# Output projection of a hybrid layer: eight whole tiles in place of a seven-product Strassen scheme

## The chip, the cores and the metric

The kernel runs on one core of one Trainium2 chip. Its time is the device time of one execution in microseconds (us); the number compared is the median of several executions. The profile shows one execution.

## What is computed

One layer on a sequence of 1024 positions and 1024 channels. What matters here is the middle of it:

```python
merged = gates[:, :, 0, :] * y_pool + gates[:, :, 1, :] * y_lru
h = h + merged @ w_out[i]                              # 1024 x 1024 x 1024
v = rms_norm(h, norm2_g[i])
g_ff, u_ff = jnp.split(v @ w_ffn_in[i], 2, axis=-1)    # D_FF = 2816
h = h + (jax.nn.silu(g_ff) * u_ff) @ w_ffn_out[i]
```

Before it stand the input projection, a pooling branch and a recurrent branch (RG-LRU), each projected to 1024 channels; after it a gated embedding and a last norm. The matrices are float32.

## The kernel before

**Operands.** Channels lie on the 128 partitions, positions along the row: an activation of 1024 channels is eight tiles of 128x1024. To keep float32 accuracy each operand x of a product is split into a rounded part (`hi`, a cast on ScalarE, line 115) and the rest (`lo`, a subtraction on VectorE, line 119), both 512 wide in one tile, and a product is three matmuls: rounded by rounded, rounded by rest, rest by rounded (`mm3`, lines 219 to 221; `mm6`, line 227, does the same for the two halves of the positions, six matmuls with each weight block used for two banks).

**Two ways to multiply.** `plain` (line 840) makes one output tile at a time: for each of the eight input tiles an `mm6`, 48 matmuls, in two units of 24, into two PSUM banks that `done` evicts. `strassen` (line 419) takes output tiles in pairs and both halves of the positions, and makes of the 2x2 blocks seven products (Winograd's form) in place of eight: 84 matmuls for a pair where `plain` has 96. It pays with sums: the operands of the weights S1 to S4 come from four subtractions or additions for each pair (line 194), those of the activations T1, T2 and T4 from lines 400 to 406, and each of the seven products has weight and activation operands of its own, that is a cast and a subtraction each. A product is added to what the others left in its bank; the evictions (`Plain`, lines 484 to 512) copy or add parts into two tiles z, which the residual then adds to x.

**Who uses which.** The input projection, the output projection, and both matrices of the SwiGLU use `strassen`; the projections of the two branches and the gate of the embedding use `plain`. In the output projection the four pairs stand in two groups of two (line 987), and each product is made for both pairs of a group before the next product. The products come in the order 1, 5, 6, 2, 7, 3, 4, for which the activation operands are B11, T1, T2, B21, T3, B22, T4.

**Order.** All engines run the order in which the program is written down, by units (one product, or half an output tile). `drive` (line 276) writes a unit after the results of the unit before it (`post`), and prepares weight operands three units ahead, loads some more. Small jobs (`background`) get a share of each unit's time. TensorE, VectorE, ScalarE and the DMA queue of SyncE each work through their own list in order and wait for each other through semaphores.

**Around the change.** `done_lru` (line 930) closes an output tile of the recurrent branch's projection: it multiplies the two banks by the gate (line 933), adds the pooling branch (934) and puts the jobs for the activation operands of the output projection in the background (937, 940). `residual` (967) closes an output tile of the output projection: adds it to x (970), stores h (88), scales it to v (974), puts the jobs for the SwiGLU's activation operands B11, T1 and T2 in the background (977, 980), and squares h on ScalarE (327) to add it to the sum of squares (328). The tiles come out in the order 0, 2, 1, 3, 4, 6, 5, 7, the last four at the end of the second group. The SwiGLU's first product needs B11 of the tiles 0, 2, 4, 6; its second T1 of the same; its third T2, for which the odd tiles are needed too. After the first product TensorE adds up the squares (345), from which VectorE and ScalarE make the norm (350 to 356, 1001, 1002); after the fourth the norm is spread over the partitions (367). The first group of the SwiGLU has three pairs, so each of its products is 3 x 12 = 36 matmuls. Tiles live in one pool of 51 buffers (line 29); a load or cast that takes over a buffer waits for its last reader.

Of the kernel before, what the change touches and what calls it, by code (L numbers as in the profile page):

```python
# [19 lines left out]
KD = D // P  # L20
# [44 lines left out]
def hybrid_block(ctx: ExitStack, tc: tile.TileContext, xT, pT, vec, w_in, w_rgig, w_pool,  # L65
# [165 lines left out]
    background = deque()  # L231
# [686 lines left out]

    ma = Acts()

# [9 lines left out]
    def done_lru(m, banks):  # L930
        g = gate_of.pop(8 + m)
        for b, s in zip(banks, (LOW, HIGH)):
            dve.tensor_mul(g[:, s], g[:, s], b)
        dve.tensor_add(g, g, t0.pop(m))
        if m % 2 == 0:
            ma.a[m // 2] = g
            background.append(some_operands(ma, m // 2, ("B11", "T1")))
        else:
            ma.b[m // 2] = g
            background.append(some_operands(ma, m // 2, ("T2", "B21")))  # L940

# [10 lines left out]

    prepare_m = prepare(ma)

    def loads_of_group(m0):
        def pre(q, j, size):
            i = QS.index(q)
            if m0 == 0:
                if i == 0 and j == 0:
                    state["ss2"] = at("ss")  # L960
                    state["rep1"] = norm1.spread()
                prepare_m(q, j, size)
            if j == 0 and i in (2, 3, 4, 5):
                load_xr(m0 + {2: 0, 3: 2, 4: 1, 5: 3}[i])
        return pre

    def residual(m):
        def then(z):
            h = xr.pop(m)
            dve.tensor_add(h, h, z)  # L970
            store(h_spill[m], h)

            v = at("v")
            dve.scalar_tensor_tensor(v, h, col(C_G2, m), state["rep1"], ALU.mult, ALU.mult)  # L974
            if m % 2 == 0:
                va.a[m // 2] = v
                background.append(some_operands(va, m // 2, ("B11", "T1")))
            else:
                va.b[m // 2] = v
                background.append(some_operands(va, m // 2, ("T2",)))  # L980
            add_square(h, state["ss2"], m == 0)
            if m == KD - 1:
                state["norm2"] = Rstd(state["ss2"])
        return then

    strassen(ma, [(w_out[2 * i], w_out[2 * i + 1]) for i in range(KD // 2)],
             lambda i: Plain(residual(2 * i), residual(2 * i + 1)), loads_of_group(0),
             last=loads_of_group(4), groups=[2, 2])


# [295 lines left out]
```

## Time and profile before

| | |
|---|---|
| median of three runs | 1426.54 us (1425.07 to 1426.93) |
| the profiled execution | 1428.4 us |
| its span, first to last instruction | 1426.7 us |
| mean granted TensorE clock | 0.978 |
| TensorE busy | 1363.4 us (96%), 5958 matmuls |
| VectorE busy | 1074.8 us (75%) |
| ScalarE busy | 697.7 us (49%) |

In the profile PE is TensorE, PEld its weight loads, DVE VectorE, ACT ScalarE, POOL GpSimd, SP SyncE with its DMA queue. L119 is line 119 of the kernel. Busy time is the sum of the instructions' spans; those of matmuls overlap, since the next one starts before the last has drained, so the pace of matmuls is read from start to start. "Idle before" an instruction is the time its engine did nothing before it, with the engine and line whose end released it. The granted clock is the share of TensorE's full 2.4 GHz; the other level is half, 1.2 GHz.

### The profile page before, as it was taken

What the parts mean: (1) busy time and instruction counts of PE and PEld (TensorE: products, weight loads), DVE (VectorE), ACT (ScalarE), POOL (GpSimd) and SP (SyncE); (2) the same over time, 40 slices, a digit from 0 to 9 for tenths busy, and PEclk for the clock granted to TensorE, in tenths of its full rate; (3) what the DMA queues carried; (4) which work ended last, traced back from release to release, by engine and by line L of the source; (5) the groups of instructions that cost most, each with busy time, mean ns of one, the idle gap of its engine ahead of it and who ended that gap; (6) DMA issues with size and microseconds to landing.
All of it is one profiled execution on the core that took longest, in us unless ns stands there. A gap on an engine that the chain in (4) does not pass through costs nothing.

```text
span 1426.7 us, 16476 instructions
## 1 busy us (share of the span) xinstructions
PE 1363.4 (96%) x5958; PEld 1117.1 (78%) x5958; DVE 1074.8 (75%) x1583; ACT 697.7 (49%) x1114; POOL 86.5 (6%) x194
## 2 busy tenths in 40 slices
PE   6999999999999999977999999999999999999986
PEld 4787888888788888756788888888888877887865
DVE  5977788888775556778798888888787856768566
ACT  6558665877866122443554444444444521226331
POOL 0003010010000000000001000111110100000000
PEclk7999999999999999989999999999999999999997
DMA  7122143333559221332024444444567798813103
GB/s 311 74 78 97 58 153 110 122 124 109 193 197 364 89 89 38 110 138 98 16 89 148 148 162 148 162 163 163 192 233 268 277 419 303 343 66 126 62 28 118
DMA packets 64738, 220.56 MB, mean 155 GB/s; under 512 B 7312, under 2 KB 9872, under 8 KB 64656
## 3 DMA queue, kind: packets, MB, share of 16 engines
q1 hardware_dynamic: 45936, 151.80, 30.0%
q0 software_dynamic: 18576, 67.64, 11.7%
q8 instruction: 47, 0.77, 0.2%
q14 instruction: 35, 0.29, 0.1%
q10 hardware_dynamic: 144, 0.06, 0.0%
HBM read 147.65 MB, written 71.83 MB: 154 GB/s over the span
## 4 chain that ended last, share of the span: by engine, by line
PE 78%; DVE 11%; ACT 5%; issue 3%; DMA 2%; POOL 1%; DVEq 0%; SPq 0%; ACTq 0%; POOLq 0%
PE ps L221 22%; PE ps L220 22%; PE ps L219 22%; PE ps L227 11%; DVE w L119 2%; DVE ss L328 1%; DVE v L974 1%; DMA wr<-w_fout 1%; DVE xr L970 1%; DMA lT<-fT 1%; DVE wr L194 1%; PE ps L367 1%; DVE xB L119 1%; ACT w L115 1%; DVE xT L119 1%
## 5 line engine op out<-in xcount | busy, mean ns | idle before, releaser
L115 ACT CAST w<-wr 128x512 fp32r<-128x512 f32 (+2 forms) x384 | 227.1, 609 | 362.6 <-DVE wr L194 252.2
L119 DVE TENSOR_TENSOR w<-wr,w 128x512 fp32r<-128x512 f32 (+2 forms) x384 | 256.5, 672 | 52.6 <-ACT w L115 51.9
L221 PE MATMUL ps<-xT,w 128*128 128x512 f32 x704 | 276.3, 392 | 9.9 <-DVE w L119 9.9
L220 PE MATMUL ps<-xT,w 128*128 128x512 f32 x704 | 275.9, 392 | 3.4 <-DVE xT L119 3.4
L219 PE MATMUL ps<-xT,w 128*128 128x512 f32 x704 | 276.0, 392 | 0.1
L220 PE MATMUL ps<-xB,w 128*128 128x512 f32 x528 | 207.6, 393 | 9.3 <-DVE xB L119 9.1
L219 PE MATMUL ps<-xB,w 128*128 128x512 f32 x528 | 206.7, 392 | 2.1 <-ACT xB L115 1.2
L221 PE MATMUL ps<-xB,w 128*128 128x512 f32 x528 | 206.9, 392 | 0.0
L221 PEld LDWEIGHTS ps<-xT,w 128*128 128x128 f32 x704 | 133.1, 189 | 40.3 <-DVE w L119 12.7
L220 PEld LDWEIGHTS ps<-xT,w 128*128 128x128 f32 x704 | 133.1, 189 | 32.5 <-DVE xT L119 5.0
L219 PEld LDWEIGHTS ps<-xT,w 128*128 128x128 f32 x704 | 133.1, 189 | 28.4 <-ACT w L115 0.7
L220 PEld LDWEIGHTS ps<-xB,w 128*128 128x128 f32 x528 | 99.8, 189 | 32.2 <-DVE xB L119 11.8
L219 PEld LDWEIGHTS ps<-xB,w 128*128 128x128 f32 x528 | 99.8, 189 | 23.8 <-ACT xB L115 1.6
L221 PEld LDWEIGHTS ps<-xB,w 128*128 128x128 f32 x528 | 100.0, 189 | 21.1 <-DVE w L119 0.6
L227 PE MATMUL ps<-y,w 128*128 128x512 f32 x384 | 87.2, 389 | 0.0
L227 PEld LDWEIGHTS ps<-y,w 128*128 128x128 f32 x384 | 72.1, 188 | 15.0
L1079 DVE TENSOR_TENSOR h<-h,ps 128x512 f32<-128x512 f32 x68 | 46.5, 684 | 42.6 <-PE ps L221 42.4
L194 DVE TENSOR_TENSOR wr<-wr 128x512 f32<-128x512 f32 (+1 forms) x112 | 76.0, 679 | 3.1 <-DMA wr<-w_fout 1.1
L219 PE MATMUL ps<-lT,w 128*128 128x512 f32 x176 | 68.9, 392 | 3.4 <-DMA lT<-fT 2.6
L221 PE MATMUL ps<-lT,w 128*128 128x512 f32 x176 | 68.7, 390 | 0.0
L220 PE MATMUL ps<-lT,w 128*128 128x512 f32 x176 | 68.5, 389 | 0.0
L115 ACT CAST w<-s 128x512 fp32r<-128x512 f32 (+1 forms) x56 | 34.3, 613 | 57.3 <-DVE s L194 57.3
(218 smaller groups left out, 2145.0 us busy)
## 6 DMA issues: line engine op xcount, KB each, us to landing
wr<-w_fin SPq DMA_DIRECT2D x44, 512.0 KB, 5.7
fT<-xT POOLq DMA_DIRECT2D x44, 512.0 KB, 5.2
lT<-fT SPq DMA_DIRECT2D x44, 512.0 KB, 8.7
wr<-w_in SPq DMA_DIRECT2D x36, 512.0 KB, 4.1
fB<-xB POOLq DMA_DIRECT2D x33, 512.0 KB, 5.7
lB<-fB SPq DMA_DIRECT2D x33, 512.0 KB, 7.7
g<-z POOLq DMA_DIRECT2D x16, 512.0 KB, 2.9
g<-g SPq DMA_DIRECT2D x16, 512.0 KB, 6.4
```

Of the source, the lines that this page charges most:

```text
L115: act.copy(op[:, :x.shape[1]], x)
L119: dve.tensor_tensor(op[:, H:H + n], x, op[:, :n].bitcast(F32), ALU.subtract)
L194: f(self.place(out), self.place(a), self.place(b))
L219: pe.matmul(bank, a, xop[:, :H], start=first, stop=False, skip_group_check=more)
L220: pe.matmul(bank, a, xop[:, H:], start=False, stop=False, skip_group_check=more)
L221: pe.matmul(bank, b, xop[:, :H], start=False, stop=last, skip_group_check=more)
L227: pe.matmul(bank, w, xop[:, s], start=f, stop=e)
L328: dve.tensor_add(ss, ss, sq)
L367: pe.matmul(bank[:, i * P:(i + 1) * P], r[:, b + i:b + i + 1].broadcast_to([P, P]), ident, start=True, stop=True)
L970: dve.tensor_add(h, h, z)
L974: dve.scalar_tensor_tensor(v, h, col(C_G2, m), state["rep1"], ALU.mult, ALU.mult)
L1079: dve.tensor_add(h[t][:, s], h[t][:, s], bank)
```

## The change

The output projection goes through `plain`: eight output tiles, one after the other (the first two interleaved by halves), eight `mm6` each, 384 matmuls. Its input tiles get their two operands (one for each half of the positions) in `done_lru` as soon as they are made (`split`). `residual` takes the two banks and adds them straight to x; the tiles come out in the order 0 to 7, so that the pairs of neighbours of which the SwiGLU's operands are made are complete one after another. The tiles of x are loaded one output tile ahead. The weights of the output projection are laid out by whole tiles in place of pairs.

```diff
--- before.py
+++ after.py
@@ -916,7 +916,7 @@
     plain([w_pproj[m] for m in range(KD)], NG, lambda: mixed, done_pproj, pre_pproj)
 
 
-    ma = Acts()
+    ms = {}
 
     def pre_lru(m, a):
         if m == 0 and a == 0:
@@ -932,12 +932,7 @@
         for b, s in zip(banks, (LOW, HIGH)):
             dve.tensor_mul(g[:, s], g[:, s], b)
         dve.tensor_add(g, g, t0.pop(m))
-        if m % 2 == 0:
-            ma.a[m // 2] = g
-            background.append(some_operands(ma, m // 2, ("B11", "T1")))
-        else:
-            ma.b[m // 2] = g
-            background.append(some_operands(ma, m // 2, ("T2", "B21")))
+        ms[m] = split(g, "m")
 
     plain([w_lru[m] for m in range(KD)], KD, lambda: ys, done_lru, pre_lru, 2)
 
@@ -950,24 +945,20 @@
         xr[m] = at("xr")
         nc.sync.dma_start(xr[m], xT[m])
 
-    prepare_m = prepare(ma)
-
-    def loads_of_group(m0):
-        def pre(q, j, size):
-            i = QS.index(q)
-            if m0 == 0:
-                if i == 0 and j == 0:
-                    state["ss2"] = at("ss")
-                    state["rep1"] = norm1.spread()
-                prepare_m(q, j, size)
-            if j == 0 and i in (2, 3, 4, 5):
-                load_xr(m0 + {2: 0, 3: 2, 4: 1, 5: 3}[i])
-        return pre
+    def pre_out(m, a):
+        if a == 0:
+            if m == 0:
+                state["ss2"] = at("ss")
+                state["rep1"] = norm1.spread()
+                load_xr(0)
+            if m + 1 < KD:
+                load_xr(m + 1)
 
     def residual(m):
         def then(z):
             h = xr.pop(m)
-            dve.tensor_add(h, h, z)
+            for b, s in zip(z, (LOW, HIGH)):
+                dve.tensor_add(h[:, s], h[:, s], b)
             store(h_spill[m], h)
 
             v = at("v")
@@ -983,9 +974,7 @@
                 state["norm2"] = Rstd(state["ss2"])
         return then
 
-    strassen(ma, [(w_out[2 * i], w_out[2 * i + 1]) for i in range(KD // 2)],
-             lambda i: Plain(residual(2 * i), residual(2 * i + 1)), loads_of_group(0),
-             last=loads_of_group(4), groups=[2, 2])
+    plain([w_out[m] for m in range(KD)], KD, lambda: ms, lambda m, banks: residual(m)(banks), pre_out, 2)
 
 
     f_spill = [spill(f"f{j}") for j in range(NJ)]
@@ -1268,7 +1257,7 @@
         "w_pool": a["pool_w"][0].transpose(1, 0, 2).reshape(P, NG * P),
         "w_pproj": tiles(a["pool_proj"][0]),
         "w_lru": tiles(a["lru_proj"][0]),
-        "w_out": tiles(pairs(a["w_out"][0])),
+        "w_out": tiles(a["w_out"][0]),
         "w_fin": tiles(pairs(a["w_ffn_in"][0])),
         "w_fout": tiles(a["w_ffn_out"][0].reshape(NJ, P, D)[blocks].reshape(DFF, D)),
         "w_pg": tiles(a["w_ple_gate"][0]),
```

**TensorE, where the output projection begins** (y are the operands of the recurrent branch's projection, the small matmuls of L367 spread the first norm, xB and xT are activation operands of a Strassen scheme, m those of the whole tiles). Before:

```order
L227 MATMUL ps<-y,w 128x512 x384
L367 MATMUL ps<-ident,sm 128x128 x8
L219 MATMUL ps<-xB_4029,w 128x512
L220 MATMUL ps<-xB_4029,w 128x512
L221 MATMUL ps<-xB_4029,w 128x512
L219 MATMUL ps<-xB_4141,w 128x512
```

With the change:

```order
L227 MATMUL ps<-y,w 128x512 x384
L367 MATMUL ps<-ident,sm 128x128 x8
L227 MATMUL ps<-m,w 128x512 x384
L219 MATMUL ps<-xB_4598,w 128x512
L220 MATMUL ps<-xB_4598,w 128x512
L221 MATMUL ps<-xB_4598,w 128x512
```

The 336 matmuls of the seven-product scheme have gone, 384 of the same form as in the stage before them stand there, and behind them the SwiGLU's first product begins (xB_4598).

**VectorE, at the closing of output tiles** (xr is the tile of x that becomes h, v the scaled tile, ss the sum of squares, w a weight operand). Before, at the first closings of the second group:

```order
L503 TENSOR_TENSOR z<-z,ps 128x512
L970 TENSOR_TENSOR xr<-xr,z 128x1024
L974 SCALAR_TENSOR_TENSOR v<-xr,cv,rstd 128x1024
L328 TENSOR_TENSOR ss<-ss,sq 128x1024
L119 TENSOR_TENSOR w<-wr,w 128x512
L503 TENSOR_TENSOR z<-z,ps 128x512
L970 TENSOR_TENSOR xr<-xr,z 128x1024
L974 SCALAR_TENSOR_TENSOR v<-xr,cv,rstd 128x1024
L328 TENSOR_TENSOR ss<-ss,sq 128x1024
L119 TENSOR_TENSOR w<-wr,w 128x512
L119 TENSOR_TENSOR xB_5078<-v,xB_5078 128x512
L400 TENSOR_TENSOR v<-v 128x512
```

With the change, tiles 4 and 5 of the projection:

```order
L961 TENSOR_TENSOR xr<-xr,ps 128x512 x2
L965 SCALAR_TENSOR_TENSOR v<-xr,cv,rstd 128x1024
L328 TENSOR_TENSOR ss<-ss,sq 128x1024
L119 TENSOR_TENSOR w<-wr,w 128x512 x2
L119 TENSOR_TENSOR xB_4865<-v,xB_4865 128x512
L400 TENSOR_TENSOR v<-v 128x512
L961 TENSOR_TENSOR xr<-xr,ps 128x512 x2
L965 SCALAR_TENSOR_TENSOR v<-xr,cv,rstd 128x1024
L328 TENSOR_TENSOR ss<-ss,sq 128x1024
L119 TENSOR_TENSOR w<-wr,w 128x512
L119 TENSOR_TENSOR xT_4900<-v,xT_4900 128x512
L403 TENSOR_TENSOR v<-v 128x512
```

The addition of z has become two additions from PSUM, and between two closings stand, in place of one weight operand, everything that a whole output tile brings.

**VectorE, at the entry of the SwiGLU.** With the change, from the closing of the last output tile on (the same list stood there before, behind the closings of four tiles that came together):

```order
L961 TENSOR_TENSOR xr<-xr,ps 128x512 x2
L965 SCALAR_TENSOR_TENSOR v<-xr,cv,rstd 128x1024
L328 TENSOR_TENSOR ss<-ss,sq 128x1024
L119 TENSOR_TENSOR w<-wr,w 128x512
L194 TENSOR_TENSOR wr<-wr 128x512 x2
L119 TENSOR_TENSOR xT_5052<-v,xT_5052 128x512
L403 TENSOR_TENSOR v<-v 128x512
L404 TENSOR_TENSOR v<-v 128x512
```

Before:

```order
L970 TENSOR_TENSOR xr<-xr,z 128x1024
L974 SCALAR_TENSOR_TENSOR v<-xr,cv,rstd 128x1024
L328 TENSOR_TENSOR ss<-ss,sq 128x1024
L119 TENSOR_TENSOR w<-wr,w 128x512
L194 TENSOR_TENSOR wr<-wr 128x512 x2
L119 TENSOR_TENSOR xT_5141<-v,xT_5141 128x512
L403 TENSOR_TENSOR v<-v 128x512
L404 TENSOR_TENSOR v<-v 128x512
```

What moved here is the place of the list: with the change TensorE's last matmul of the projection stands right before it, and three tiles have been closed earlier.

## Rows read from the trace of the kernel before

**Rows 1.** The page: busy us, share of the span and number of instructions.

```profile
PE 1363.4 (96%) x5958; PEld 1117.1 (78%) x5958; DVE 1074.8 (75%) x1583; ACT 697.7 (49%) x1114; POOL 86.5 (6%) x194
```

**Rows 2.** Stretches: length, PE, PEld, DVE, ACT, POOL busy (x), granted clock, DMA, GB/s.

```profile
473.70:560.90 87.20, 87.20 (x386) 72.23 (x385) 50.55 (x74) 14.75 (x26) 0.00 (x0) 1.00 0.22 73
562.60:655.70 93.10, 81.86 (x339) 65.64 (x338) 72.15 (x100) 40.61 (x70) 3.19 (x6) 0.95 0.36 124
655.70:703.60 47.90, 38.96 (x177) 31.45 (x176) 40.12 (x65) 24.11 (x43) 1.06 (x2) 0.93 0.08 33
```

**Rows 3.** Timeline of PE at the borders of the stages: start us, us, instruction.

```profile
562.64 0.48 PE L219 MATMUL ps<-xB,w 128*128 128x512 f32 x1
...
655.71 0.39 PE L219 MATMUL ps<-xB,w 128*128 128x512 f32 x1
...
674.09 0.50 PE L345 MATMUL ps<-mean,ss 128*128 128x1 f32 x4
...
675.79 0.49 PE L219 MATMUL ps<-xT,w 128*128 128x512 f32 x1
...
693.11 0.39 PE L219 MATMUL ps<-xB,w 128*128 128x512 f32 x1
...
701.33 0.38 PE L367 MATMUL ps<-ident,ratio 128*128 128x128 f32 x2
...
703.61 0.48 PE L219 MATMUL ps<-xT,w 128*128 128x512 f32 x1
```

**Rows 4.** The same timeline, where PE stood longest; idle before in brackets.

```profile
614.35 0.50 PE L221 MATMUL ps<-xT,w 128*128 128x512 f32 x1 [3.79 <-DVE w L119]
...
623.62 0.80 PE L221 MATMUL ps<-xT,w 128*128 128x512 f32 x1 [4.64 <-DVE w L119]
...
666.49 0.80 PE L220 MATMUL ps<-xB,w 128*128 128x512 f32 x1 [7.19 <-DVE xB L119]
```

**Rows 5.** Groups by line and shape, 473.7 to 560.9: xcount | busy us, mean ns | idle.

```profile
L227 PE MATMUL ps<-y,w 128*128 128x512 f32 x384 | 87.2, 389 | 0.0
...
L933 DVE TENSOR_TENSOR g<-g,ps 128x512 f32<-128x512 f32 x14 | 9.0, 684 | 32.7 <-PE ps L227 32.7
L934 DVE TENSOR_TENSOR g<-g 128x1024 f32<-128x1024 f32 x7 | 8.6, 1226 | 0.2
```

**Rows 6.** The same view of DVE, 562.6 to 703.7.

```profile
L119 DVE TENSOR_TENSOR w<-wr,w 128x512 fp32r<-128x512 f32 x34 | 23.3, 687 | 7.7 <-ACT w L115 7.7
L974 DVE SCALAR_TENSOR_TENSOR v<-xr,cv,rstd 128x1024 f32<-128x1024 f32 x8 | 10.3, 1285 | 0.4
L970 DVE TENSOR_TENSOR xr<-xr,z 128x1024 f32<-128x1024 f32 x8 | 9.8, 1226 | 3.7 <-ACT z L509 3.6
L328 DVE TENSOR_TENSOR ss<-ss,sq 128x1024 f32<-128x1024 f32 x7 | 8.5, 1218 | 0.0
...
L194 DVE TENSOR_TENSOR wr<-wr 128x512 f32<-128x512 f32 x10 | 6.9, 688 | 0.2
...
L503 DVE TENSOR_TENSOR z<-z,ps 128x512 f32<-128x512 f32 x4 | 2.7, 682 | 1.4 <-PE ps L221 1.4
```

**Rows 7.** Timeline of DVE from the last closing to the third sum of the SwiGLU.

```profile
669.41 1.23 DVE L970 TENSOR_TENSOR xr<-xr,z 128x1024 f32<-128x1024 f32 x1 [0.57 <-ACT z L509]
...
686.34 0.68 DVE L119 TENSOR_TENSOR xT<-v,xT 128x512 fp32r<-128x512 f32 x1
686.94 0.68 DVE L119 TENSOR_TENSOR w<-s,w 128x512 fp32r<-128x512 f32 x1
...
701.96 0.69 DVE L1020 TENSOR_TENSOR fg<-fg,ps 128x512 f32<-128x512 f32 x1
```

**Rows 8.** The loads of w_fin, from issue to landing.

```profile
DMA to landing us min/median/max: 3.3/5.7/7.9
```

**Rows 9.** Who PE waited for from 703 to the end: us, times, longest.

```profile
PE ps L219 <- DMA lT<-fT: 2.6, 2, 1.5
```

## The prediction

> **What bounds the kernel now.** I read the page first: TensorE is busy 96% of the span, VectorE 75% [rows 1]. That is a mean over stages, so the next view is the busy time by stretch [rows 2]. The projection of the recurrent branch (473.7 to 560.9) shows what a stage looks like that TensorE bounds: busy all the time, full clock, VectorE at 50.6 of 87.2 us. The output projection (562.6 to 655.7) is another thing: TensorE is busy 81.9 of 93.1 us at a mean granted clock of 0.95, and VectorE 72.2 us. The entry of the SwiGLU (655.7 to 703.6) goes on in the same way: 39.0 of 47.9 us, clock 0.93, VectorE 40.1. So in these 141 us TensorE, the bound of the kernel as a whole, stands and waits. The timeline says for whom: the long stops before 614, 623 and 666 us (3.8, 4.6 and 7.2 us) end each with a VectorE instruction of line 119, the rest of a weight or of an activation operand [rows 4]. The clock falls in the same two stretches, and the instructions behind the stops at 623 and 666 last 0.80 us where one at full clock is listed with 0.39 [rows 3, 4].
>
> How much is lost there follows from the pace. 384 matmuls take 87.2 us in the undisturbed stage, 0.227 each [rows 5]; the 36 between 693.11 and 701.33 take 0.228 each [rows 3], so the other form of matmul has the same pace. The seven-product scheme has 7 x 4 x 12 = 336, worth 76.3 us; the stage took 562.64 to 655.71 = 93.1 [rows 3], so 16.8 are lost. The entry has 36 matmuls, the sums of the norm (674.09 to 675.79, 1.7 us), 72 matmuls, 36 more, and the spreading of the norm (701.33 to 703.61, 2.3 us) [rows 3]: 144 x 0.227 + 4.0 = 36.7 us, against 47.9, so 11.2 are lost.
>
> **Matmuls.** 384 in place of 336, so 48 x 0.227 = 10.9 us more work on TensorE. All of it is on the path: nothing else covers a matmul.
>
> **VectorE's load in the projection.** Removed: 16 sums of weights, 16 of activations, and the rests of 12 weight and 12 activation operands, 56 instructions at 0.69 us [rows 6], 38.5 us. The evictions had 12 half additions from PSUM (0.682) and 8 whole additions of z (1.226), 18.0 us; now 16 halves, 10.9. Together 45.6 us less on VectorE. ScalarE loses 24 casts and 16 copies; it did not bound anything here and I give that nothing.
>
> Does VectorE still bind? For each output tile it now has two additions (1.36), the scaling (1.29), the sum of squares (1.22), two weight rests (1.37), and of the SwiGLU's operands, for two tiles, three rests and three sums (4.1, so 2.06 for one): 7.3 us [rows 6], against 48 x 0.227 = 10.9 us of TensorE. It keeps a third of its time free, the tiles close one by one, and weight operands are three units of 5.4 us ahead. So I take the stage at TensorE's pace: 384 x 0.227 = 87.2 us. The bounds: 87.2 below; above, with the 16.8 us lost before added again, 104.0. I take the lower end because the row nearest to it is a stage of the same form, the same number of matmuls and 5 us of VectorE work per tile, that lost nothing [rows 2, 5].
>
> **The operands made in the stage before.** Two casts and two rests per tile come behind the gate's products: two half products (0.684), one addition (1.226) [rows 5], then four steps of about 0.69, 5.4 us; with two weight rests VectorE then works some 5.3 us per 10.9. Hidden by TensorE's work. The last tile's bank is complete at 560.9, its operands at about 566.3, and TensorE asks for tiles 4 to 7 only after the first halves of output tiles 0 and 1, at 562.6 + 10.9 = 573.5. Cost 0; without this cover each us late would be one us.
>
> **The entry of the SwiGLU.** Before, four closings came together (tiles 4, 6, 5, 7), the last one at 669.4, 13.7 us behind the end of the projection [rows 3, 7]. Now only tile 7 is left at that point. VectorE's list from the last closing on is nearly the same, and its length is measured: from 669.41 to the third sum of the SwiGLU's pairs at 701.96, 32.6 us [rows 7]. TensorE needs to the end of the product before that sum 36 + 72 + 36 matmuls and the norm's sums, 34.4 us. So it becomes slightly longer than VectorE's list. The tightest operand inside is the rest of the second weight of the third product: ready 17.5 + 0.7 = 18.2 us behind the last closing [rows 7], asked for after 8.2 + 1.7 + 8.2 + 2.7 = 20.8. I take the entry at 36.7 us; the bounds are 36.7 and the 47.9 of before.
>
> **Loads.** As many, of the same size. A load of w_fin landed 3.3 to 7.9 us after its issue [rows 8]. They are issued six weight operands ahead, which is now 6 x 5.4 us. But the 16 operand tiles now live through the whole stage in the pool of 51 buffers, and a load waits for a buffer's last reader; so one load late at the entry is an unknown between 0 and 7.9 us. I take 0, since the raw weights mostly take over buffers of closed output tiles.
>
> **The sum.** Before, 562.64 to 703.61: 141.0 us. After: 87.2 + 36.7 = 123.9. The difference is 17.1 us. What follows has the same list of instructions, so it moves forward as a whole. The profiled execution took 1428.4 us, which gives 1411.3; it lies 1.9 above the median of 1426.54, so for the median I say 1409.4.
>
> **The rivals.**
>
> *The entry stays late.* VectorE's list and TensorE's work at the entry differ by 1.8 us only. If ScalarE's casts between them or a late load hold VectorE up, the entry takes its 47.9 us again and only the projection gains, 93.1 - 87.2 = 5.9: 1420.6. For it: VectorE is busy 40.1 of 47.9 us there now [rows 2]. Against it: three of four closings are gone from its front. 10%; part of this loss is likelier than all of it.
>
> *Slower: TensorE binds and the stops stay.* If the stops come from the closings, not from the Strassen operands, they stay, and 10.9 us of matmuls come on top: 1437.4. For it: every closing costs VectorE 1.23 + 1.29 + 1.22 us in a row, and these eight chains remain. It decides from the point where VectorE has more than 10.9 us of work for each output tile; the rows give 7.3. 5%. The Trainium skill (Perfetto Trace Analysis, Identifying the Most-Contended Engine) would have the engine with the highest occupancy relieved first; that is TensorE, and by this rule a change that gives it 48 matmuls more loses those 10.9 us. The same page (Optimization Strategy) allows that this engine changes over time, and the stretches of [rows 2] are such a case.
>
> *The gain is swallowed later.* The last stages read spilled operands back, and TensorE waits there for a DMA now and then, but for 2.6 us in all [rows 9]. If loads became the bound there, up to the whole gain would go: 1426.5. These loads are issued by the same list, behind the same buffers' readers, so they move too. 3%.
>
> **How the numbers follow.** 82% for the forecast, with its smaller losses; 10, 5 and 3% for the rivals. 0.2%, 2.9 us, is about what a measurement of this kernel can tell from no change. Faster: the forecast, the late entry, and half of the swallowed gain, 0.93; same 0.02, slower 0.05. The range: below, 1406.5, which would need the 2.3 us of spreading and a few tenths elsewhere to shrink too; above, 1416.5, the forecast and one load or operand late by some 7 us. That leaves out most of the rivals, 18%.
>
> **What the profile of the changed kernel would show.** Right: a group of 384 matmuls of the output projection with some 87 us and almost no idle time; granted clock 1.00 from 562 to 686; the first matmul of the SwiGLU near 650 and the end of the norm's spreading near 686. VectorE waits for TensorE at the closings of output tiles. Wrong: stops of TensorE over 2 us in front of an operand's rest (the entry), idle time inside the projection's group (VectorE still binds), or the fourth product at its place but the end not 17 us earlier (swallowed later).

## The result and the profile after

The changed kernel took **1409.58 us** (median of four runs, 1408.02 to 1409.92), the kernel before 1426.74 on the same chip (four runs, 1425.07 to 1428.16): ratio 0.9877, 95% interval 0.9865 to 0.989, 17.2 us less. The prediction was 1409.4, range 1406.5 to 1416.5.

First the page of the changed kernel: busy time and share of the span (1407.8 us), and the group of the output projection's matmuls.

```profile
PE 1364.6 (97%) x6006; PEld 1121.5 (80%) x6006; DVE 1032.6 (73%) x1523; ACT 675.3 (48%) x1074; POOL 86.5 (6%) x194
...
L227 PE MATMUL ps<-m,w 128*128 128x512 f32 x384 | 87.3, 389 | 0.0
```

Against [rows 1]: 48 matmuls more on TensorE, 60 instructions and 42.2 us less on VectorE. The 384 matmuls of the projection have no idle time. The stretches, with the columns of [rows 2]: the recurrent branch's projection, the output projection, the entry of the SwiGLU to the end of the norm's spreading, and the rest.

```profile
472.20:559.43 87.23, 87.23 (x386) 72.23 (x385) 42.38 (x62) 14.77 (x27) 0.00 (x0) 1.00 0.32 109
561.13:648.29 87.16, 87.16 (x387) 72.17 (x386) 50.70 (x69) 24.32 (x38) 3.72 (x7) 1.00 0.31 109
648.29:684.92 36.63, 36.45 (x178) 30.59 (x176) 27.92 (x49) 18.64 (x33) 0.53 (x1) 1.00 0.04 15
684.92:1407.80 722.88, 699.98 (x3087) 576.87 (x3085) 549.90 (x842) 286.85 (x487) 40.91 (x77) 0.98 0.48 179
```

The last stretch of the kernel before, cut at the same place of the program (it answers to the fourth row):

```profile
703.61:1426.70 723.09, 700.11 (x3087) 576.83 (x3085) 550.13 (x842) 286.87 (x487) 40.91 (x77) 0.98 0.48 179
```

So 141.0 us of [rows 3] became 87.16 + 36.63 = 123.8, at a granted clock of 1.00, and what follows takes the same 723 us. The two spans differ by 18.9: these 17.2, and 1.5 in which the changed kernel was ahead when the output projection began. That is not the change's: in the run below with the order 4, 6, 5, 7, whose code ahead of this point is the change's, it lies at 563.6. Kernels are therefore compared here by the **stretch** from the first matmul of the output projection to the end of the norm's spreading: 123.8 in the changed kernel, and 123.8 again in a second run of it (1409.64 us).

TensorE's timeline at the entry, and all that it waited for from 560 to 700 (engine, line <- releaser: us, times, longest):

```profile
648.29 0.39 PE L219 MATMUL ps<-xB,w 128*128 128x512 f32 x1
...
656.45 1.84 PE L345 MATMUL ps<-mean,ss 128*128 128x1 f32 x16
658.15 0.49 PE L219 MATMUL ps<-xT,w 128*128 128x512 f32 x1
...
674.62 0.39 PE L219 MATMUL ps<-xB,w 128*128 128x512 f32 x1
...
682.78 1.05 PE L367 MATMUL ps<-ident,ratio 128*128 128x128 f32 x8
...
684.92 0.48 PE L219 MATMUL ps<-xT,w 128*128 128x512 f32 x1
```

```profile
PE ps L367 <- DVE fg L1009: 0.2, 1, 0.2
```

The stops of [rows 4] have gone. Who waits now is VectorE. Its timeline at the last two closings:

```profile
637.38 1.28 DVE L961 TENSOR_TENSOR xr<-xr,ps 128x512 f32<-128x512 f32 x2 [3.41 <-PE ps L227]
...
643.58 0.69 DVE L119 TENSOR_TENSOR xB<-v,xB 128x512 fp32r<-128x512 f32 x1
644.29 0.69 DVE L400 TENSOR_TENSOR v<-v 128x512 f32<-128x512 f32 x1
648.26 1.28 DVE L961 TENSOR_TENSOR xr<-xr,ps 128x512 f32<-128x512 f32 x2 [3.28 <-PE ps L227]
...
665.21 0.68 DVE L119 TENSOR_TENSOR w<-s,w 128x512 fp32r<-128x512 f32 x1
```

The closings are 10.9 us apart, VectorE is idle 3.3 us before each, and the rest of B11 of tile 6 (643.58) is ready 4 us before the SwiGLU asks for its first operands.

### The profile page after: what moved, and what is told of

Its sections match the earlier page's. It is cut to its first block, busy times and chain, and to the rows that moved or that the text cites. A ratio compares the mean times of both kernels' runs of the same rounds, so it can differ in the third digit from the quotient of the medians.

```text
span 1407.8 us, 16468 instructions
## 1 busy us (share of the span) xinstructions
PE 1364.6 (97%) x6006; PEld 1121.5 (80%) x6006; DVE 1032.6 (73%) x1523; ACT 675.3 (48%) x1074; POOL 86.5 (6%) x194
## 3 DMA queue, kind: packets, MB, share of 16 engines
q0 software_dynamic: 18576, 67.64, 11.9%
## 4 chain that ended last, share of the span: by engine, by line
PE 85%; DVE 6%; ACT 4%; issue 3%; DMA 1%; POOL 1%; DVEq 0%; SPq 0%; ACTq 0%; POOLq 0%
PE ps L221 22%; PE ps L219 22%; PE ps L220 22%; PE ps L227 17%; DVE w L119 1%; DVE ss L328 1%; DMA lT<-fT 1%; PE ps L367 1%; PE ps L345 1%; DVE pg L1139 0%; ACT pg L1137 0%; DVE h L1140 0%; ACT sq L1145 0%; DVE pg L1136 0%; DMA x<-xT 0%
## 5 line engine op out<-in xcount | busy, mean ns | idle before, releaser
L115 ACT CAST w<-wr 128x512 fp32r<-128x512 f32 (+2 forms) x376 | 221.6, 608 | 339.9 <-DVE wr L194 245.0
L119 DVE TENSOR_TENSOR w<-wr,w 128x512 fp32r<-128x512 f32 (+2 forms) x376 | 249.9, 671 | 44.2 <-ACT w L115 43.4
L221 PE MATMUL ps<-xT,w 128*128 128x512 f32 x640 | 249.5, 390 | 1.5 <-DVE w L119 1.4
L219 PE MATMUL ps<-xT,w 128*128 128x512 f32 x640 | 249.4, 390 | 0.1
L220 PE MATMUL ps<-xT,w 128*128 128x512 f32 x640 | 249.1, 389 | 0.0
L219 PE MATMUL ps<-xB,w 128*128 128x512 f32 x480 | 187.2, 390 | 2.1 <-ACT xB L115 1.2
L220 PE MATMUL ps<-xB,w 128*128 128x512 f32 x480 | 187.4, 391 | 1.9 <-DVE xB L119 1.9
L221 PE MATMUL ps<-xB,w 128*128 128x512 f32 x480 | 187.4, 390 | 0.0
L221 PEld LDWEIGHTS ps<-xT,w 128*128 128x128 f32 x640 | 120.1, 188 | 28.1 <-DVE w L119 3.2
L219 PEld LDWEIGHTS ps<-xT,w 128*128 128x128 f32 x640 | 120.2, 188 | 25.1 <-ACT w L115 0.5
L220 PEld LDWEIGHTS ps<-xT,w 128*128 128x128 f32 x640 | 120.1, 188 | 25.1
L220 PEld LDWEIGHTS ps<-xB,w 128*128 128x128 f32 x480 | 90.3, 188 | 21.8 <-DVE xB L119 3.1
L219 PEld LDWEIGHTS ps<-xB,w 128*128 128x128 f32 x480 | 90.2, 188 | 21.5 <-ACT xB L115 1.6
L221 PEld LDWEIGHTS ps<-xB,w 128*128 128x128 f32 x480 | 90.3, 188 | 19.2 <-DVE w L119 0.6
L227 PE MATMUL ps<-m,w 128*128 128x512 f32 x384 | 87.3, 389 | 0.0
L227 PE MATMUL ps<-y,w 128*128 128x512 f32 x384 | 87.2, 389 | 0.0
L227 PEld LDWEIGHTS ps<-y,w 128*128 128x128 f32 x384 | 72.1, 188 | 15.0
L227 PEld LDWEIGHTS ps<-m,w 128*128 128x128 f32 x384 | 72.0, 188 | 14.9
L1068 DVE TENSOR_TENSOR h<-h,ps 128x512 f32<-128x512 f32 x68 | 46.5, 684 | 42.5 <-PE ps L221 42.4
L194 DVE TENSOR_TENSOR wr<-wr 128x512 f32<-128x512 f32 (+1 forms) x104 | 70.4, 678 | 3.0 <-DMA wr<-w_fout 1.2
L219 PE MATMUL ps<-lT,w 128*128 128x512 f32 x176 | 69.0, 392 | 3.4 <-DMA lT<-fT 2.7
L221 PE MATMUL ps<-lT,w 128*128 128x512 f32 x176 | 68.7, 390 | 0.0
```

What stands on the lines that cost most here:

```text
L115: act.copy(op[:, :x.shape[1]], x)
L119: dve.tensor_tensor(op[:, H:H + n], x, op[:, :n].bitcast(F32), ALU.subtract)
L194: f(self.place(out), self.place(a), self.place(b))
L219: pe.matmul(bank, a, xop[:, :H], start=first, stop=False, skip_group_check=more)
L220: pe.matmul(bank, a, xop[:, H:], start=False, stop=False, skip_group_check=more)
L221: pe.matmul(bank, b, xop[:, :H], start=False, stop=last, skip_group_check=more)
```

## The experiments

That the time went out of these two stages is plain. Why TensorE had stood there is not, and the prediction gave one reason for each stage. Theory 1: the **amount** of VectorE's work; TensorE stands when VectorE has more to do than fits beside the matmuls. Theory 2: the **order** in VectorE's list; closings come several in a row, and the rests that TensorE needs next stand behind them. (The expectations also name a theory 3, that the form of the seven products and their shared banks makes the loss. The loss that whole tiles show below, 10.3 us in the projection with more work and 9.5 at the entry with closings together, needs no such form.) All times are set against runs of the kernel before on the same chip (1427.15 us beside the two runs with more work, the order 4, 5, 6, 7 and the groups 2, 1, 1; 1427.4 beside the order 4, 6, 5, 7, the two runs on the sums and the two sets of operands; 1426.62 beside the rest).

### More work for VectorE

In the changed kernel the scaling of each output tile is written three times, or six times, the same result each time.

```diff
-            dve.scalar_tensor_tensor(v, h, col(C_G2, m), state["rep1"], ALU.mult, ALU.mult)
+            for _ in range(1 + 2):
+                dve.scalar_tensor_tensor(v, h, col(C_G2, m), state["rep1"], ALU.mult, ALU.mult)
```

Three times:

> The changed kernel, with the scaling of each closed output tile (v) written three times instead of once: the same values, 16 whole instructions more on VectorE, 1.2 to 1.3 us each, about 2.5 us per output tile. Theory 1, VectorE's load per tile against TensorE's 10.9 us decides: 7.3 + 2.5 = 9.8 is still under 10.9, so the projection stays at 87.2 us (within 0.5); VectorE's list at the entry grows from 32.6 to 35.1 us against TensorE's 34.4, so the entry takes 0 to 1.5 us more. In all 0 to +1.5 us against the changed kernel. Theory 2, closings that come together at the end made the loss: 0 to +1. Theory 3, the seven-product form of the matmuls and its shared banks made the loss: 0.

Six times:

> The same with the scaling written six times: 40 instructions more, about 6.2 us per tile, 50 us in all, some more than the 45.6 us that the change took off VectorE. Theory 1: 7.3 + 6.2 = 13.5 us per tile against 10.9: VectorE falls behind by 2.6 us a tile, first hidden by weight operands made three units ahead (up to 16 us), then seen as stops of TensorE late in the projection and at the entry: +10 to +22 us against the changed kernel. Theory 2: only the last closing counts, 6.2 us longer against 1.8 us to spare: about +4.5. Theory 3: 0.

Three times: 1409.90 us, ratio 0.9877 (0.9848 to 0.9906), no different from the change alone. Six times: 1438.67, ratio 1.0079 (1.0049 to 1.0108). The two stretches of each, three times first:

```profile
561.40:648.60 87.20, 87.20 (x387) 72.22 (x387) 68.55 (x83) 24.73 (x38) 3.72 (x7) 1.00 0.31 109
648.60:685.20 36.60, 36.42 (x178) 30.56 (x176) 30.37 (x51) 18.54 (x33) 0.53 (x1) 1.00 0.04 15
```

```profile
561.07:658.54 97.47, 90.83 (x387) 73.93 (x386) 82.85 (x91) 21.60 (x34) 3.30 (x7) 0.96 0.28 93
658.54:713.10 54.56, 42.83 (x177) 34.78 (x176) 46.53 (x67) 21.72 (x38) 0.95 (x2) 0.84 0.05 20
```

With 7.3 + 2 x 1.28 = 9.9 us of VectorE for each output tile nothing is lost; with 7.3 + 5 x 1.28 = 13.7, over the 10.9 of TensorE, 28.2 us are, 17.9 of them at the entry, where VectorE is still behind. (VectorE works there without a pause: its closings from 603.30 to 656.85 follow each other after 13.4 us.) So the amount does decide, from a point between 9.9 and 13.7. The kernel before was near it: its VectorE was busy 72.1 of 93.1 us (77%), but TensorE's own work there is 76.3 us, and 72.1 are 95% of that. The three-times kernel, with 68.6 of 87.2 (79%), loses nothing. So these runs alone don't tell whether the amount or the order made the loss.

### Closings together

The last four output tiles side by side (first halves 4, 5, 6, 7, then second halves), so that they close together; then the same in the order 4, 6, 5, 7. VectorE's instructions are those of the change.

```diff
-        seq += [(m, a) for m in range(side, len(srcs)) for a, b in parts]
+        seq += [(m, a) for m in range(side, len(srcs) - tail) for a, b in parts]
+        seq += [(m, a) for a, b in parts for m in range(len(srcs) - tail, len(srcs))]
...
+        seq += [(m, a) for a, b in parts for m in (4, 6, 5, 7)[:tail]]
```

The order 4, 5, 6, 7:

> The changed kernel with the last four output tiles side by side (first halves of tiles 4 to 7, then second halves): closings of 4 to 7 come 5.4 us apart, each needs 3.7 to 3.9 us of VectorE for itself and 1.4 for weights; total work unchanged. Theory 1: VectorE keeps up with the closings but the operands of the SwiGLU (about 8 us of work) pile up behind them, 1.8 us of it to spare: entry 2 to 7 us longer, projection 87.2. Theory 2: most of the 11.2 us that the entry lost before come back: +8 to +11. Theory 3: 0.

The order 4, 6, 5, 7:

> As the run with the last four output tiles side by side, but in the order 4, 6, 5, 7, so that tile 6, the last one that the SwiGLU's first product needs, closes 10.9 us before the end as in the changed kernel and not 5.4. The number of closings at the end is the same as in that run. Theory 2a, what counts is how long before the entry the last even tile closes: the 10 us of that run mostly go, +0 to +4 us against the changed kernel. Theory 2b, four closings near each other delay all that stands behind them: +8 to +10 as in that run.

4, 5, 6, 7: 1420.02 us, ratio 0.9949 (0.9926 to 0.9971), 10.4 slower than the change. The two stretches, then VectorE's timeline, then TensorE's two stops:

```profile
561.45:648.61 87.16, 87.16 (x388) 72.18 (x386) 45.56 (x61) 22.51 (x35) 3.73 (x7) 1.00 0.27 96
648.61:694.70 46.09, 38.43 (x176) 31.54 (x175) 33.40 (x57) 20.96 (x37) 0.53 (x1) 0.93 0.06 24
```

```profile
646.29 1.28 DVE L962 TENSOR_TENSOR xr<-xr,ps 128x512 f32<-128x512 f32 x2
...
652.48 1.28 DVE L962 TENSOR_TENSOR xr<-xr,ps 128x512 f32<-128x512 f32 x2
653.79 1.28 DVE L966 SCALAR_TENSOR_TENSOR v<-xr,cv,rstd 128x1024 f32<-128x1024 f32 x1
654.99 1.22 DVE L328 TENSOR_TENSOR ss<-ss,sq 128x1024 f32<-128x1024 f32 x1
...
658.06 0.68 DVE L119 TENSOR_TENSOR xB<-v,xB 128x512 fp32r<-128x512 f32 x1
```

```profile
653.23 0.50 PE L219 MATMUL ps<-xB,w 128*128 128x512 f32 x1 [2.42 <-ACT xB L115]
658.80 0.79 PE L220 MATMUL ps<-xB,w 128*128 128x512 f32 x1 [5.07 <-DVE xB L119]
```

The projection keeps its 87.2 us; the entry takes 46.1 in place of 36.6. VectorE has no instruction more in the two stretches together (118 in both kernels); eight of them, 5.5 us, have moved from the projection into the entry. Tile 6 closes at 646.29, but its B11 (658.06) stands behind the closing of tile 7, and TensorE's second stop ends with it. This is the entry of the kernel before (47.9), made again with whole tiles. The order 4, 6, 5, 7 has a stretch of 124.9 us, 1.1 over the change, with one stop of 0.6; it took 1414.48 us, ratio 0.9908 (0.9888 to 0.9928), and of these 4.9 us over the change 2.5 lie ahead of the stretch in its profiled execution. Its entry, then VectorE's rest of B11 of tile 6 and the closing of tile 7:

```profile
650.79:688.57 37.78, 36.85 (x178) 30.43 (x176) 31.88 (x56) 20.39 (x36) 0.53 (x1) 1.00 0.04 15
```

```profile
651.30 0.68 DVE L119 TENSOR_TENSOR xB<-v,xB 128x512 fp32r<-128x512 f32 x1
...
654.31 1.28 DVE L962 TENSOR_TENSOR xr<-xr,ps 128x512 f32<-128x512 f32 x2
```

There too the four close together, and VectorE has one instruction less in the entry than with 4, 5, 6, 7 (56 and 57), yet the entry is 8.3 us shorter; B11 of tile 6 stands ahead of the last closing. What counts at the entry is where the next operand stands, not that tiles close together.

### Less work for VectorE in the kernel before

The other way round: VectorE is relieved in the kernel before, first of the 32 sums of the seven-product scheme (these operands then hold other data).

```diff
-    ma = Acts()
+    ma = Acts(sums=False)
...
-             last=loads_of_group(4), groups=[2, 2])
+             last=loads_of_group(4), groups=[2, 2], sums=False)
```

> The kernel before, seven products, 336 matmuls, casts and rests as they were, but with the 32 sums of the output projection left out (the operands are then made of one block each; this part of the computation is left out). Theory 1: VectorE has 22 us less to do, the projection's 16.8 us of loss shrink by 8 to 16 us; the entry, which has closings together, keeps 8 to 11. In all -8 to -17 us against the kernel before. Theory 3, the form of the products and their shared banks make the loss: 0 to -2.

Then of the addition of the squares of tiles 1 to 7, which stands within the closings:

```diff
-            add_square(h, state["ss2"], m == 0)
+            if m == 0:
+                add_square(h, state["ss2"], True)
```

> The kernel before without the sum of squares of the output tiles 1 to 7 (part of the computation is left out: their squares on ScalarE and their seven additions on VectorE, 1.22 us each). That is 8.5 us less on VectorE, a third of what the run without the 32 sums took away, but all of it in the closings. Theory bunch (the stops are the closings in a row in front of the next rests): a closing costs VectorE 2.5 in place of 3.7 us, four in a row 4.9 less, so the stops before 614 and 623 and the one at 666 shrink by 1 to 4 us each, and the time falls by 7 to 9 us against the kernel before. Theory amount (only the sum of VectorE's work counts): 8.5/22 of the 5.9 us which those sums gave, so 2 us.

Without the sums 1422.98 us, ratio 0.9971 (0.996 to 0.9982), 4.4 us less than the kernel before, which lies in neither theory's range (8 to 17, and 0 to 2); with short closings 1420.96, ratio 0.9961 (0.9946 to 0.9976). The stretches, without sums first:

```profile
563.49:650.40 86.91, 80.02 (x339) 64.77 (x338) 60.92 (x82) 38.97 (x68) 3.19 (x6) 0.96 0.39 133
650.40:698.57 48.17, 39.92 (x178) 32.53 (x176) 40.22 (x65) 24.10 (x43) 1.06 (x2) 0.89 0.08 33
```

```profile
563.02:652.68 89.66, 80.40 (x340) 64.68 (x339) 68.69 (x98) 36.72 (x66) 3.19 (x6) 0.96 0.37 133
652.68:696.14 43.46, 38.34 (x177) 31.65 (x176) 35.65 (x60) 20.90 (x38) 1.06 (x2) 0.96 0.07 28
```

Of the 32 sums 14 were made in the stage before; in the projection 18 instructions and 11.2 us of VectorE's busy time have gone (72.1 in [rows 2] to 60.9), and it is 6.2 us shorter (93.1 to 86.9). VectorE's 60.9 us are 80% of TensorE's own 76.3, and 10.6 us are still lost: this is what speaks against the amount alone. Nothing was taken from the entry, and it stays at 48. The seven additions are 3.4 us of VectorE in the projection and 4.5 in the entry, and these are 3.4 and 4.4 us shorter. So a microsecond taken from a closing came back whole, one taken from the sums by half. (The seven squares that ScalarE is spared too don't explain it: VectorE waits as long for ScalarE's copies of z, 3.6 us, and its casts of weights, 9.1 and 9.2 us, as before.) My bound for the amount alone in the second run (2 us) was set too low, since I counted all 32 sums: by the 18 it is 7.9/11.2 x 6.2 = 4.4. The stretch (141.0 to 133.1, one execution of each) speaks for the closings; the medians, 5.7 us less with an interval of 3.4 to 7.7, don't tell 4.4 from 7.9.

How a closing makes a stop is seen at the stop before 614 of [rows 4], in VectorE's timeline of the kernel before:

```profile
609.95 1.23 DVE L970 TENSOR_TENSOR xr<-xr,z 128x1024 f32<-128x1024 f32 x1 [1.23 <-ACT z L509]
611.28 1.28 DVE L974 SCALAR_TENSOR_TENSOR v<-xr,cv,rstd 128x1024 f32<-128x1024 f32 x1
612.48 1.22 DVE L328 TENSOR_TENSOR ss<-ss,sq 128x1024 f32<-128x1024 f32 x1
613.61 0.68 DVE L119 TENSOR_TENSOR w<-wr,w 128x512 fp32r<-128x512 f32 x1
```

The closing first waits for ScalarE's copy of z, and the rest of the weight that TensorE wants stands behind it. VectorE, the late engine, is idle just before. With short closings this stop went from 3.8 to 1.4 us, that at the entry from 7.2 to 4.9; the one before 623, which I had expected to shrink too, did not (4.6 before, 5.1 here): TensorE came there earlier and waited for the same kind of rest.

### Two attempts to mend the kernel before

The groups 2, 1, 1 in place of 2, 2, so that pairs close apart; and the sums on GpSimd.

```diff
-             last=loads_of_group(4), groups=[2, 2])
+             last=loads_of_group(6), groups=[2, 1, 1], mid=loads_of_group(4))
```

> The kernel before, seven-product scheme kept, with groups of two, one and one pairs instead of two and two: the same instructions on VectorE but the closings of tiles 4 and 5 come 19 us before those of 6 and 7. Theory 1: VectorE's load in the projection is the same, so the projection keeps most of its 16.8 us of loss and the entry gives back a part: 0 to -8 us against the kernel before. Theory 2: the entry loses nothing any more, -9 to -11 us, and the projection keeps only what stood in the first group. Theory 3: 0.

```diff
-    ma = Acts()
+    ma = Acts(eng=pool)
...
-             last=loads_of_group(4), groups=[2, 2])
+             last=loads_of_group(4), groups=[2, 2], eng=pool)
```

> The kernel before, with the 32 sums of the output projection's operands (16 of weights, 16 of activations) made by GpSimd instead of VectorE; results the same. Theory 1, VectorE's amount of work decides: it loses 32 x 0.69 = 22 us, some 15 of them inside the 141 us of projection and entry; if GpSimd works beside it, -8 to -15 us against the kernel before. Rival: GpSimd is so slow with a sum, or holds VectorE up so much, that the operands come later than before: 0 or slower. Theory 2, closings together: the entry keeps its 11.2 us in any case.

The groups 2, 1, 1 took 1441.95 us, ratio 1.0102 (1.0054 to 1.0149), slower by 15, which neither theory had said: the edit made a new wait, the first row here (what TensorE waited for, 560 to 720). With one pair in a group the next product needs the same bank, which ScalarE copies out behind all it has in its own list. So its time decides nothing between the theories. Its entry does speak to theory 2, which wanted no loss there: TensorE still stops for 6.1 us before 680.50, since with tiles 6 and 7 in one group the rest of B11 of tile 6 (679.76) again stands behind the closing of tile 7 (674.24).

```profile
PE ps L219 <- ACT z L499: 18.8, 2, 12.4
```

The sums on GpSimd took 1429.60 us, ratio 1.002 (1.0009 to 1.003). GpSimd's groups in the stretch (xcount | busy, mean ns), two groups of VectorE there (its rests of weights and the sum of squares, L119 and L328 in [rows 6]), and TensorE's largest wait:

```profile
L196 POOL TENSOR_TENSOR wr<-wr 128x512 f32<-128x512 f32 x4 | 7.5, 1864 | 0.2
...
L196 POOL TENSOR_TENSOR wr<-wr,s 128x512 f32<-128x512 f32 x4 | 5.8, 1449 | 10.1 <-DVE w L119 10.1
```

```profile
L119 DVE TENSOR_TENSOR w<-wr,w 128x512 fp32r<-128x512 f32 x34 | 32.0, 943 | 3.8 <-ACT w L115 3.8
L330 DVE TENSOR_TENSOR ss<-ss,sq 128x1024 f32<-128x1024 f32 x7 | 11.7, 1678 | 0.0
```

```profile
PE ps L223 <- DVE w L119: 12.1, 3, 6.0
```

The same sums take 1.3 to 1.9 us there (means of the groups) for the 0.69 of [rows 6], and a sum stands in the chain from raw weight to rest. But VectorE was not relieved either: its own rests and sums of squares last longer while GpSimd works. Ten of the 34 rests run beside a sum on GpSimd and take 1.56 us on average, the others 0.69; three of the seven sums of squares take 2.29 us, the others 1.22. That is 11.9 us more in these two groups than in [rows 6], about as much as the sums that left VectorE in the projection (11.2), so with 18 instructions fewer it is busy 73.4 us there after 72.1. The longest stop, 6.0 us before 615.65, ends with such a pair: a sum of squares of 2.28 us and a rest of 1.74. So the rival of the expectation, that GpSimd holds VectorE up, is what the trace shows, and the run says nothing on the amount.

### Half whole tiles

The first two pairs by the seven-product scheme, the last four tiles whole: 360 matmuls, 5.4 us less than the change. In the first version the whole tiles have operands of their own:

```diff
-    plain([w_out[m] for m in range(KD)], KD, lambda: ms, lambda m, banks: residual(m)(banks), pre_out, 2)
+    strassen(ma, [(w_out[2 * i], w_out[2 * i + 1]) for i in range(2)],
+             lambda i: Plain(residual(2 * i), residual(2 * i + 1)), pre_first, groups=[2])
+    plain([w_out[4 + m] for m in range(4)], KD, lambda: ms, lambda m, banks: residual(4 + m)(banks),
+          pre_rest)
```

> The first two pairs of output tiles by the seven-product scheme in one group, the last four tiles whole: 168 + 192 = 360 matmuls, 24 less than in the changed kernel (5.4 us). The first group lost 3.8 us in the kernel before. Theory 1 and 2: 38.1 + 3.8 + 43.5 + an entry of 36.7 = 122.1 against 123.8 of the changed kernel: -1.7 us (0 to -4). Rival: both sets of operands (28 and 16 tiles) fill the pool of 51 buffers, loads come late, and VectorE makes both sets: +3 to +15 us.

In the second they take over B11, B21 and B22 of the scheme and add one operand B12; in the third T3, B22 and T4 of the first six input tiles are also made in the stage before:

```diff
+        return {2 * k + i: tuple(ma.op[n, k] for n in ns) for k in range(4)
+                for i, ns in enumerate((("B11", "B12"), ("B21", "B22")))}
...
+            background.append(some_operands(ma, m // 2, ("B11", "T1", "B12")))
...
-            background.append(some_operands(ma, m // 2, ("T2", "B21"), True))
+            background.append(some_operands(ma, m // 2, ("T2", "B21", "T3", "B22", "T4") if m < 6 else ("T2", "B21"), True))
```

> The first four output tiles by the seven-product scheme in one group of two pairs, the last four as whole tiles; these take over the operands that the scheme has already (B11, B21, B22) and add only one more for each of the four pairs of input tiles, so VectorE has 12 rests (8.2 us) less in the first group than in the run that made both sets. 360 matmuls in place of 384, 5.4 us less than in the change. Theory bunch: the stops in the first group (6 us of 45.4) come from the double set; without it the group takes 38.1 to 41.9, the whole tiles 43.5 and the entry 36.6 as before, together 118 to 122, so 2 to 5 us less than the change. The rival: the closings 0, 2, 1, 3 and the scheme's sums keep the group at 44 or more, no gain or up to 2 us slower than the change.

> As the run with the shared operands, and the activation operands T3, B22, T4 of the input tiles 0 to 5 are made in the stage before, where VectorE is free for 40 us in 100: 9 rests and 3 sums, 8.3 us, leave the first group. Expected: the first group at 38.1 to 40, and 1 to 3 us faster than the run with the shared operands alone. The rival: these early jobs stand in VectorE's list in front of B11 and T1 of the last input tiles, and the group starts late: 2 to 5 us slower than with the shared operands alone.

The change was run again beside the last two:

> The changed kernel again, for the comparison with the two versions of half whole tiles on the same chip: 1409 to 1411 us.

| | us | ratio to before | stretch |
|---|---|---|---|
| two sets of operands | 1412.73 | 0.9893 (0.9876 to 0.9909) | 125.5 |
| shared operands | 1408.95 | 0.9877 (0.986 to 0.9893) | 121.7 |
| shared, and early | 1406.41 | 0.9858 (0.9843 to 0.9872) | 120.0 |
| the change again | 1409.64 | 0.9885 (0.9868 to 0.9901) | 123.8 |

With two sets the first group took 45.4 us for 168 x 0.227 = 38.1; the stretch came out 1.7 us longer than the change's, where 1.7 less was expected. The stretches of the last version: first group, whole tiles, entry.

```profile
562.21:602.08 39.87, 39.07 (x172) 31.47 (x171) 30.29 (x45) 19.12 (x34) 1.06 (x2) 1.00 0.38 127
602.08:645.60 43.52, 43.52 (x194) 36.04 (x193) 38.91 (x52) 17.07 (x27) 2.66 (x5) 1.00 0.52 186
645.60:682.23 36.63, 36.45 (x178) 30.59 (x176) 27.93 (x49) 18.63 (x33) 0.53 (x1) 1.00 0.04 15
```

It is the fastest kernel here: its four runs (1405.07 to 1407.67) all lie below those of the change beside it (1408.62 to 1413.14). Sharing alone gained 2.1 us of stretch; by the medians it can't be told from the change. The middle row shows again that a high load alone makes no loss: VectorE is busy 38.9 of 43.5 us (89%), closes five tiles there, and TensorE loses nothing. Two of these closings, of a scheme's tile and of the first whole tile, and a rest of a weight between them:

```profile
614.05 1.23 DVE L981 TENSOR_TENSOR xr<-xr,z 128x1024 f32<-128x1024 f32 x1 [0.57 <-ACT z L510]
...
617.65 0.68 DVE L119 TENSOR_TENSOR w<-wr,w 128x512 fp32r<-128x512 f32 x1
...
621.39 1.28 DVE L984 TENSOR_TENSOR xr<-xr,ps 128x512 f32<-128x512 f32 x2
```

The first whole tile's banks are complete at 602.08 + 48 x 0.227 = 613.0; its closing comes 8 us late, and no one waits, since the operands that TensorE needs meanwhile have been made earlier.

How much earlier is a third thing that the change altered, beside amount and order: the **lead**. A weight's rest is written three units ahead of the unit that uses it. A unit of the scheme is 12 matmuls, so the lead is 36 x 0.227 = 8.2 us; a unit of a whole tile is 24, so it is 16.3 us, and TensorE needs a new weight half as often. In the program's order the rest at 617.65 is that of the fourth unit here, which begins at 602.08 + 72 x 0.227 = 618.4: ready just in time. In the kernel before, the closing at 609.95 was as late (its last product ended at 601.8), the rest at 613.61 behind it belonged to the unit that began at 610.0, and TensorE stood for 3.8 us. No run changes the lead alone, so what it is worth in the projection is not shown.

## Why the prediction was right, point by point

- **Matmuls**, +10.9 us all on the path: right; 87.16 us for 384.
- **VectorE's load**, -45.6 us: measured -42.2. The 60 instructions were counted right; the durations were too long, since VectorE's instructions in a row overlap and a busy time counts an overlap once. (It is not the sum of the spans: 384 matmuls listed with 389 ns are 87.2 us in [rows 5].) In the timeline of the change the sums and rests at 654.57, 655.18 and 655.78, listed with 0.68 and 0.69, follow each other after 0.61 and 0.60.
- **Does VectorE still bind?** No, as said: 7.3 us for a tile against 10.9 (the stage has 50.7 us of VectorE, 6.3 for a tile), and the three-times run shows that 9.9 would do as well. But for the 16.8 us lost before, the section names only that load, and the load alone doesn't make them: set against TensorE's own matmuls it was 95% before; without the sums it is 80%, and 10.6 us are still lost, while 79% (scaling three times) and 89% (half whole, early) lost nothing. Without the sums 6.2 came back, half of what VectorE was relieved of. That the tiles close one by one and that a unit is now 5.4 us long stand in the section beside the load, without a price. The short closings show that the first counts; what the second is worth is open. The second rival of the prediction was right in that stops come from the closings, and wrong in what it drew from it: they don't stay when the closings are spread and the weights have more lead.
- **The part that the prediction never priced**: of the 28.0 us lost before, TensorE is idle for 20.2 (93.10 - 81.86 and 47.90 - 38.96 in [rows 2]), and 5.6 are 31 matmuls behind stops that follow each other after 0.33 to 0.5 us in place of 0.227 (the granted clock of 0.95 and 0.93 in [rows 2]; the 0.80 us instructions in [rows 4] begin such runs). The remaining 2.2 lie in the matmuls next to the stops. Adding all lost time at once took it in without naming it.
- **Operands in the stage before**, cost 0: right. The stage keeps its 87.2 us; VectorE is busy 42.4 of them, 5.3 for each 10.9, as worked out.
- **The entry**, 36.7 us for 47.9: 36.63. Here the reason was the right one, and the closings side by side show it: the same instructions in another order cost 9.5 us. The tightest rest was to be ready 18.2 us behind the last closing and asked for after 20.8. It starts at 665.21 and ends 17.6 behind 648.26; the product's second weight is due at 658.15 + 36 x 0.227 + 2.7 = 669.0, after 20.8.
- **Loads**, 0: right; TensorE's list of waits has no DMA in it.
- **The sum**, -17.1: -17.2. What follows takes 722.9 after 723.1, so the rival of the swallowed gain fell.
- **The busiest engine.** TensorE had 96% of the span before, got 48 matmuls more, has 97% now, and the time fell by 17.2 us. The Trainium skill (Perfetto Trace Analysis, Identifying the Most-Contended Engine) says to optimize the engine of the highest occupancy first, and to judge TensorE's headroom by its share of the peak rate or by the busy share of its weight loads; by busy time and by weight loads (96% and 78%, VectorE 75%, [rows 1]) that is TensorE. Read as giving this engine less work, as the prediction read it, the rule would have kept the seven products, and in this stretch the measurement decides against that reading. What the change took away were that same engine's stops.

What stays open is how the projection's 16.8 us divide between amount, order and lead. Shorter closings gave 3.4 of them, no sums 6.2; no run took away both, and 7.2 would be left if they add up. The stop before 623 yielded to neither by much. The lead of the weights was varied by no run alone. At the entry the cause is shown: there the same whole tiles in another order make most of the loss and take it away.

## What to carry to other kernels

When the busiest engine stops for an in-order engine that isn't full, look at what stands in that engine's list just ahead of the awaited instruction, and whether that was itself waiting. Compare how late that engine can get with how far ahead the operand is made. Spreading out such blocks, or making the awaited operand earlier, can pay for extra work on the busiest engine: here 10.9 us of matmuls bought back 28.0 us of lost time. Then ask which part of the saving scheme can come back where its operands are made under cover: half of it did, for another 3.2 us.

## What the runs showed of the hardware that I had not expected

- A stop costs more than its length. After a stop of 5.1 us in the run with short closings, TensorE's timeline goes on like this:

```profile
620.42 0.79 PE L221 MATMUL ps<-xT,w 128*128 128x512 f32 x1 [5.09 <-DVE w L119]
621.02 0.63 PE L219 MATMUL ps<-xT,w 128*128 128x512 f32 x1
621.44 0.63 PE L220 MATMUL ps<-xT,w 128*128 128x512 f32 x1
...
626.11 0.40 PE L219 MATMUL ps<-xT,w 128*128 128x512 f32 x1
```

The columns of [rows 2] for these matmuls:

```profile
621.02:626.10 5.08, 5.08 (x13) 3.96 (x12) 4.31 (x8) 3.63 (x7) 0.00 (x0) 0.50 0.33 107
```

Thirteen matmuls follow each other after 0.40 to 0.60 us, most after 0.43, at a granted clock of 0.50, the lower of the two levels, and only then after 0.227 again. With the scaling six times I had expected 10 to 22 us more than the change and measured 29; some 6 of these are such matmuls.
- VectorE's instructions of 0.69 us follow each other after 0.60 to 0.61 us.
- GpSimd takes 1.3 to 1.9 us for a sum of 128x512 that takes VectorE 0.69, and beside such sums VectorE's rests of weights took 1.56 us on average in place of 0.69.
